# Feeding the down product's first operands at earlier places in the order of work

## The chip, the cores and the metric

The kernel runs on one core of a Trainium2 chip. The metric is the device time of one execution in microseconds (us). A core has five engines with queues of their own, which run each in its own order and wait for each other by semaphores: TensorE (PE, matmuls), VectorE (DVE), ScalarE (ACT), GpSimd (POOL) and SyncE (SP). SP and POOL here only start transfers (DMA) between the chip's large memory and the on-chip buffers. Matmuls write to eight accumulation banks ("bank"), from which VectorE and ScalarE read.

## The reference: two layers, each with a feed-forward block

The reference takes x (1024 positions by 1024 channels, float32) through two layers. Layer 0 mixes by a short gated convolution, layer 1 by a dilated attention. Behind each mixer comes the feed-forward block that matters here:

```python
def swiglu(h, w_gate, w_up, w_down):
    return (jax.nn.silu(h @ w_gate) * (h @ w_up)) @ w_down
...
        h = rms_norm(x, ffn_norm[i])
        x = x + swiglu(h, ffn_w_gate[i], ffn_w_up[i], ffn_w_down[i])
    return rms_norm(x, final_norm)
```

The inner width is 2816, 22 tiles of 128 rows.

## The kernel before

**Products in three parts.** Every float32 matrix is split into a high part (a rounded copy) and a low part (what is left), and a product is three matmuls: high by high, high by low, low by high (lines 505 to 507 in `mm`, 597 to 600 in `deeper`). The copy is made by ScalarE (line 137 for weights `w`, line 497 for operands `b`), and VectorE subtracts it to get the low part (lines 138 and 498). Each split so puts one instruction on ScalarE and one on VectorE.

**Seven products for eight.** The large products use Winograd's form of Strassen's scheme. A pair of weight tiles (a *unit*) is multiplied in seven products, m = 1, 2, 6, 5, 7, 3, 4 (`WINOGRAD`), and every product has an operand of its own made from the quarters of the activations, kept in `self.b[m]`. Gate and up have 22 units, 0 to 21. For units from 4 on, products 2 and 4 are themselves done by such a scheme on half-width pieces, for two units at a time; these are called *deep* products here, `(unit, DEEPER + i)` in the order of work, i = 1, 2, 5, 6, 7, 3, 4. After each deep product VectorE adds its two banks to stored parts (line 515).

**The order around the change.** `unit_order` writes it out by hand. At its end stand, for units 20 and 21: (20, 6), (20, 5), (20, 7), (21, 1), (20, 3), (21, 6), (21, 5), (21, 7), deep 1, deep 2, deep 5, deep 6, (21, 3), deep 7, deep 3, deep 4. Below, "sixth product", "fifth product" and so on mean (21, 6), (21, 5), and so on, by their number m and not by their place. A whole product is 12 matmuls of 512 columns, a deep one 12 of 256. Several products share one bank: deep 4 accumulates in the bank that deep 7 has filled, once VectorE has read it.

**The down product.** It reads the product of gate and up, of which 18 of the 22 tiles go through the seven-product scheme, in three chunks of three pairs. The quarters' sums were written to the large memory when they were made. `feed` (line 695) is a generator for one chunk: each call loads the three pieces of one operand (`hin`, line 702, on SP's queue) and then converts the three pieces loaded by the call before (ScalarE line 497, VectorE line 498), so eight calls load and convert all seven operands. `down` (line 719) then runs, for each m, the product for two output tiles, n and n + 2; after each VectorE adds the bank into the residual x (line 726), and the feed is called once. The products m = 1, 6, 7 and 4 share a bank: m = 6 can start only when m = 1's add has read it. Weights for down come by `load_raw` (line 151, SP's queue too) and are split a few products ahead by `ensure`.

**Where the feed starts.** The method `run` of class `Strassen` calls `filled(n)` after product number n of the gate and up order. Before the change, it calls the feed for the products of unit 21 that stand at deep 6 or behind it, five products.

**Buffers.** `hin`, the sums of weight tiles (`combo`), the parts of gate and up and some deep operands come from one pool of 20 half-page buffers; `b`, `w`, `raw` and `x` from 41 pages. A buffer that is written again waits for the last reader of what was in it. Instructions of each engine run in the order in which the program names them.

The block runs twice, once in each layer, with the same order of work.

Of the kernel before, what the change touches and what calls it, by code (L numbers as in the profile page):

```python
# [30 lines left out]
DEEP, DEEPER = (2, 4), 10  # L31
# [10 lines left out]
CONV = "conv"  # L42
# [52 lines left out]
def trunk(ctx: ExitStack, tc: tile.TileContext, x, gains_in, cwi, ck, cwo, wqkv, wo, relb,  # L95
# [62 lines left out]
    def ensure(upto):  # L158
        while op_state[0] < min(upto + 1, len(ops)):
            key = ops[op_state[0] + 1][0] if op_state[0] + 1 < len(ops) else None  # L160
            if key in sums_of:
                sums_of.pop(key)()
            made[op_state[0]] = ops[op_state[0]][1]()
            op_state[0] += 1
# [49 lines left out]
    def add_deep(unit, key, u, rows, upto):  # L214
# [27 lines left out]
        def early(op):  # L242
            w = op()
            run(*[sums_of(j, m) for j, m in enumerate(DEEP)])
            return w
# [105 lines left out]
    def run(*gens):  # L351
        for _ in zip(*gens):
            pass
        for g in gens:
            for _ in g:
                pass
# [6 lines left out]
    def both(w, ks, acts):  # L363
        banks = two_banks()
        run(product(w, ks, acts, banks))
        return banks
# [106 lines left out]
    class Strassen:  # L473
# [277 lines left out]
        def run(self, start, hooks={}):  # L751

            self.base = op_state[1]
            last = self.nu - 1

            def filled(n):
                start(n)
                if self.key != CONV:
                    self.now = n + 1
                    i = self.order.index((3, 4))  # L760
                    if n == i - 15:
                        prep.append(self.deepen(2))
                    if n == i - 5:
                        prep.append(self.deepen(4))
                    for p in prep:
                        next(p, None)
                if self.key == CONV:
                    self.below(n, last)
                else:
                    if self.order[n][0] == last and n >= self.at(last, DEEPER + 6) - self.base:  # L770
                        next(feed, None)
                    if self.order[n] == (last, DEEPER + 7):
                        self.load_x(0, 2)
                        ensure(self.at(last, DEEPER + 4) + 4)
                self.idle(n)

            prep = []
            if self.key == CONV:
                self.products(filled, hooks)
                self.first_tiles()  # L780
                return
            feed = self.feed(0)
            self.products(filled, hooks)
            for c in range(0, self.pairs, self.chunk):
                self.down(c, 0, feed)
                feed = self.feed(c + self.chunk) if c + self.chunk < self.pairs else self.feed_last()
                self.down(c, 4, feed)
            run(feed)


    class Conv(Strassen):
# [148 lines left out]
        def first_tiles(self):  # L940

            run(self.low)
            upper = self.halved(range(CO, KT))
            for n in range(KT):
                banks = two_banks()
                run(product(take(("co", 0, n), 2), range(CO), self.hid, banks))
                if n + 2 < KT:
                    self.load_x(n + 2)
                add_to_x(n, banks)
                self.step(4 if n < 2 else None)  # L950
                if n >= 3:
                    next(upper, None)
            run(upper)
            for f in range(CO):
                del self.plain[f]
# [843 lines left out]
```

## Time and profile before

| | us |
|---|---|
| median of three runs | 2215.94 |
| lowest and highest | 2215.3 and 2217.3 |
| profiled execution, its own time | 2215.37 |
| its span in the profile | 2213.6 |
| TensorE busy | 2143.2 (97%) |
| VectorE busy | 1769.8 (80%) |
| ScalarE busy | 998.4 (45%) |

How to read the rows. A row of a timeline gives the start in us from the span's begin, the duration, the engine, the line of the kernel, the operation, what it writes and reads by the program's names, how many instructions were merged, and in brackets the idle time of the engine ahead of it and what ended it. A row of waits gives who waited for whom: us in total, how often, the longest. Who ended a wait is inferred; where an instruction waits for several things, the one that came last by the profile is named. A row of windows gives a stretch, its length, for TensorE busy time and number of matmuls, the clock that was granted to TensorE (1.00 is full), the DMA engines' busy share and GB/s. On VectorE and ScalarE the instructions overlap a little: the time from one start to the next is shorter than the duration of one.

### The profile page before, as it was taken

How to read it: one execution, taken by the hardware profiler on the slowest of the kernel's cores; microseconds unless marked ns; L12 is line 12 of the kernel's file. 1: busy time of each engine (PE TensorE's matmuls, PEld its weight loads, DVE VectorE, ACT ScalarE, POOL GpSimd, SP SyncE). 2: the span in 40 equal slices, each digit the busy share in tenths (PEclk: the TensorE clock that was granted, in tenths of full speed). 3: DMA queues.
4: the chain of work that ended last, by engine and by line, in shares of the span. 5: the costliest groups of instructions: out<-in, count | busy, mean ns of one | idle time of the engine just before them, and what ended most of it. 6: DMA issues, size and time to landing. Idle time of an engine off the chain costs nothing.

```text
span 2213.6 us, 30526 instructions
## 1 busy us (share of the span) xinstructions
PE 2143.2 (97%) x11138; PEld 1829.8 (83%) x11138; DVE 1769.8 (80%) x3255; ACT 998.4 (45%) x1808; POOL 147.9 (7%) x196
## 2 busy tenths in 40 slices
PE   7899999899999999999999999999899999999998
PEld 5788887688888878878999999887678888878887
DVE  7797758888888798965677767868988888889886
ACT  6433425444444444434455555534534444444435
POOL 0000000010101000010111111110010101000000
PEclk9999999999999999999999999999999999999999
DMA  4122541222323374423333333544113323266432
GB/s 154 53 84 74 208 131 51 86 98 90 117 93 114 106 269 153 131 86 131 90 90 91 90 90 83 168 130 140 62 72 102 113 96 119 96 218 210 155 93 77
DMA packets 131263, 255.30 MB, mean 115 GB/s; under 512 B 47386, under 2 KB 58666, under 8 KB 131114
## 3 DMA queue, kind: packets, MB, share of 16 engines
q1 hardware_dynamic: 75978, 184.80, 26.2%
q0 software_dynamic: 13968, 45.46, 5.6%
q10 hardware_dynamic: 41168, 23.10, 3.6%
q8 instruction: 88, 1.44, 0.3%
q14 instruction: 61, 0.50, 0.1%
HBM read 187.04 MB, written 66.26 MB: 114 GB/s over the span
## 4 chain that ended last, share of the span: by engine, by line
PE 79%; DVE 11%; ACT 4%; DMA 3%; issue 2%; ACTq 0%; SPq 0%; DVEq 0%
PE bank L505 16%; PE bank L507 16%; PE bank L506 16%; PE bank L346 5%; PE bank L348 5%; PE bank L347 5%; PE bank L1425 4%; PE bank L600 2%; PE bank L599 2%; PE bank L597 2%; DVE b L498 2%; DVE w L138 2%; PE bank L1353 1%; PE bank L1352 1%; DVE x L438 1%
## 5 line engine op out<-in xcount | busy, mean ns | idle before, releaser
L505 PE MATMUL bank<-b,w 128*128 128x512 f32 x1784 | 706.1, 396 | 27.2 <-DVE part L515 7.3
L507 PE MATMUL bank<-b,w 128*128 128x512 f32 x1784 | 702.7, 394 | 15.8 <-DVE w L138 15.8
L506 PE MATMUL bank<-b,w 128*128 128x512 f32 x1784 | 702.7, 394 | 2.1 <-DVE b L498 2.1
L505 PEld LDWEIGHTS bank<-b,w 128*128 128x128 f32 x1784 | 339.8, 190 | 102.4 <-ACT w L137 10.5
L507 PEld LDWEIGHTS bank<-b,w 128*128 128x128 f32 x1784 | 339.4, 190 | 91.9 <-DVE w L138 20.3
L506 PEld LDWEIGHTS bank<-b,w 128*128 128x128 f32 x1784 | 340.0, 191 | 73.3 <-DVE b L498 2.9
L137 ACT ACTIVATE w<-combo 128x512 fp32r<-128x512 f32 (+2 forms) x464 | 235.0, 535 | 279.2 <-DVE combo L185 273.4
L138 DVE TENSOR_TENSOR w<-combo,w 128x512 fp32r<-128x512 f32 (+2 forms) x464 | 260.6, 575 | 69.2 <-ACT w L137 67.2
L511 ACT ACTIVATE part<-bank 128x512 f32<-128x512 f32 x168 | 99.2, 594 | 276.1 <-PE bank L507 273.6
L138 DVE TENSOR_TENSOR w<-raw,w 128x512 fp32r<-128x512 f32 (+2 forms) x316 | 168.9, 559 | 20.8 <-ACT w L137 19.1
L515 DVE TENSOR_TENSOR part<-part,bank 128x256 f32<-128x256 f32 (+1 forms) x348 | 158.6, 486 | 31.0 <-PE bank L507 15.5
L137 ACT ACTIVATE w<-raw 128x512 fp32r<-128x512 f32 (+2 forms) x316 | 150.2, 520 | 45.7 <-PE bank L507 11.3
L726 DVE TENSOR_TENSOR x<-x,bank 128x512 f32<-128x512 f32 x168 | 114.2, 680 | 30.9 <-PE bank L507 30.9
L346 PE MATMUL bank<-w_hi,w 128*128 128x512 f32 (+1 forms) x320 | 122.0, 381 | 0.0
L348 PE MATMUL bank<-w_hi,w 128*128 128x512 f32 (+1 forms) x320 | 120.0, 375 | 0.7 <-DVE w L138 0.7
L347 PE MATMUL bank<-w_lo,w 128*128 128x512 f32 (+1 forms) x320 | 119.8, 374 | 0.0
L438 DVE TENSOR_TENSOR x<-x,bank 128x512 f32<-128x512 f32 (+1 forms) x104 | 65.9, 641 | 62.6 <-PE bank L348 53.8
L185 DVE TENSOR_TENSOR combo<-raw 128x512 f32<-128x512 f32 (+1 forms) x160 | 102.9, 643 | 4.3 <-DMA raw<-in_conv_w_in 4.3
L346 PE MATMUL bank<-h_hi,w_hi 128*128 128x512 f32 x256 | 104.6, 409 | 0.7 <-ACT w_hi L137 0.7
L348 PE MATMUL bank<-h_hi,w_lo 128*128 128x512 f32 x256 | 100.2, 391 | 0.7 <-DVE w_lo L138 0.7
L347 PE MATMUL bank<-h_lo,w_hi 128*128 128x512 f32 x256 | 99.9, 390 | 0.0
L1111 ACT ACTIVATE part<-part 128x512 f32<-128x512 f32 x66 | 39.7, 628 | 110.6 <-DVE part L515 110.6
(237 smaller groups left out, 3835.2 us busy)
## 6 DMA issues: line engine op xcount, KB each, us to landing
hin<-part SPq DMA_DIRECT2D x126, 256.0 KB
raw<-in_ffn_w_gate SPq DMA_DIRECT2D x44, 512.0 KB
raw<-in_ffn_w_up SPq DMA_DIRECT2D x44, 512.0 KB
part<-sum POOLq DMA_DIRECT2D x72, 256.0 KB, 3.0
raw<-in_ffn_w_down SPq DMA_DIRECT2D x48, 384.0 KB
x<-spill SPq DMA_DIRECT2D x24, 512.0 KB
raw<-in_attn_w_qkv SPq DMA_DIRECT2D x24, 512.0 KB
raw<-in_conv_w_in SPq DMA_DIRECT2D x21, 512.0 KB
```

What stands on the lines that cost most here:

```text
L137: nc.scalar.activation(hi, src, AF.Copy)
L138: eng.tensor_tensor(out=lo, in0=src, in1=hi, op=ALU.subtract)
L185: eng.tensor_tensor(out=c, in0=a, in1=b, op=op)
L346: nc.tensor.matmul(b, whi[:, a], ahi[:, s], start=first, stop=False)
L347: nc.tensor.matmul(b, whi[:, a], alo[:, s], start=False, stop=False)
L348: nc.tensor.matmul(b, wlo[:, a], ahi[:, s], start=False, stop=last)
L505: nc.tensor.matmul(b, hi[:, a], bhi, start=start and k == 0, stop=False, skip_group_check=True)
L506: nc.tensor.matmul(b, hi[:, a], blo, start=False, stop=False, skip_group_check=True)
L507: nc.tensor.matmul(b, lo[:, a], bhi, start=False, stop=k == n - 1, skip_group_check=True)
L511: nc.scalar.activation(t, b, AF.Copy)
L515: nc.vector.tensor_tensor(out=t, in0=t, in1=b, op=ALU.add)
L726: nc.vector.tensor_tensor(out=X[n][:, half(h)], in0=X[n][:, half(h)], in1=b, op=ALU.add)
```

## The change

The feed of the first chunk is called at other places in the gate and up order of the last unit. Before, it was called after every product of unit 21 from deep 6 on. After, it is called after every product from (21, 6) on but deep 5 and deep 6; this takes in every entry of the order from there, and all of them belong to unit 21.

```diff
                 if self.key == CONV:
                     self.below(n, last)
                 else:
-                    if self.order[n][0] == last and n >= self.at(last, DEEPER + 6) - self.base:
+                    if n in feeding:
                         next(feed, None)
                     if self.order[n] == (last, DEEPER + 7):
                         self.load_x(0, 2)
...
             prep = []
+
+            feeding = [n for n, um in enumerate(self.order) if n >= self.order.index((last, 6))
+                       and um not in ((last, DEEPER + 5), (last, DEEPER + 6))] if self.key != CONV else ()
             if self.key == CONV:
```

The calls stand so, with what each one loads and converts:

| call | before, after | after the change, after | loads operand | converts operand |
|---|---|---|---|---|
| 1 | deep 6 | (21, 6) | 1 | - |
| 2 | (21, 3) | (21, 5) | 2 | 1 |
| 3 | deep 7 | (21, 7) | 6 | 2 |
| 4 | deep 3 | deep 1 | 5 | 6 |
| 5 | deep 4 | deep 2 | 7 | 5 |
| 6 | down, m = 1 | (21, 3) | 3 | 7 |
| 7 | down, m = 2 | deep 7 | 4 | 3 |
| 8 | down, m = 6 | deep 3 | - | 4 |

A ninth call, after deep 4, and those in the first part of the down product find the feed at its end and do nothing. The other chunks are fed as before.

## The prediction

> **What bounds the kernel now.** I read the page first, then the waits of TensorE (PE) in the two feed-forward blocks, then VectorE's (DVE) timeline there, then windows of busy time and clock.
>
> ```profile
> span 2213.6 us, 30526 instructions
> ...
> PE 2143.2 (97%) x11138; PEld 1829.8 (83%) x11138; DVE 1769.8 (80%) x3255; ACT 998.4 (45%) x1808; POOL 147.9 (7%) x196
> ...
> PE 79%; DVE 11%; ACT 4%; DMA 3%; issue 2%; ACTq 0%; SPq 0%; DVEq 0%
> ...
> part<-sum POOLq DMA_DIRECT2D x72, 256.0 KB, 3.0
> ```
>
> TensorE is busy 97% of the span and is 79% of the chain that ended last, so a change is worth what it does to TensorE's idle time. The place that the change touches has two idle stretches in each feed-forward block. TensorE's waits from 735 to 830 us and from 1925 to 2155 us, and the rows of the first pair:
>
> ```profile
> PE bank L505 <- ACT b L497: 3.0, 1, 3.0
> PE bank L597 <- DVE part L515: 2.0, 1, 2.0
> ...
> PE bank L505 <- ACT b L497: 3.0, 1, 3.0
> PE bank L597 <- ACT b L497: 2.0, 1, 2.0
> ```
>
> ```profile
> 786.21 0.36 PE L597 MATMUL bank<-t,w 128*128 128x256 f32 x1 [2.01 <-DVE part L515]
> ...
> 795.68 0.39 PE L507 MATMUL bank<-b,w 128*128 128x512 f32 x1
> 799.08 0.71 PE L505 MATMUL bank<-b,w 128*128 128x512 f32 x1 [3.01 <-ACT b L497]
> ```
>
> The first (2.01) stands before deep product 4 of the last unit, the second (3.01) before the down product's third step, m = 6 of output tile 0. Two releasers are named ACT b L497, a conversion of a later operand, on which nothing here depends. By the code, deep 4 accumulates in the bank that deep 7's add (L515) must have read, and m = 6 in the bank that m = 1's add into x (L726) must have read. VectorE's timeline agrees:
>
> ```profile
> 769.12 1.43 DVE L138 TENSOR_TENSOR w<-raw,w 128x256 fp32r<-128x256 f32 x4
> 770.48 0.75 DVE L138 TENSOR_TENSOR w<-combo,w 128x256 fp32r<-128x256 f32 x2
> 773.50 0.69 DVE L583 TENSOR_TENSOR c<-part,bank 128x512 f32<-128x512 f32 x1 [2.28 <-ACT part L511]
> 774.23 0.69 DVE L1114 TENSOR_TENSOR c<-c,c 128x512 f32<-128x512 f32 x1
> ...
> 777.38 0.74 DVE L515 TENSOR_TENSOR part<-part,bank 128x256 f32<-128x256 f32 x2
> 778.04 0.75 DVE L138 TENSOR_TENSOR w<-combo,w 128x256 fp32r<-128x256 f32 x2
> ...
> 781.38 0.69 DVE L515 TENSOR_TENSOR part<-part,bank 128x512 f32<-128x512 f32 x1 [0.59 <-PE bank L507]
> 782.10 0.69 DVE L1114 TENSOR_TENSOR part<-part 128x512 f32<-128x512 f32 x1
> 782.71 1.89 DVE L498 TENSOR_TENSOR b<-hin,b 128x512 fp32r<-128x512 f32 x3
> 784.51 1.22 DVE L138 TENSOR_TENSOR w<-raw,w 128x256 fp32r<-128x256 f32 x3
> 785.65 0.75 DVE L515 TENSOR_TENSOR part<-part,bank 128x256 f32<-128x256 f32 x2
> 786.32 1.89 DVE L498 TENSOR_TENSOR b<-hin,b 128x512 fp32r<-128x512 f32 x3
> ...
> 791.25 1.89 DVE L498 TENSOR_TENSOR b<-hin,b 128x512 fp32r<-128x512 f32 x3
> ...
> 794.92 1.89 DVE L498 TENSOR_TENSOR b<-hin,b 128x512 fp32r<-128x512 f32 x3
> ...
> 798.25 0.68 DVE L726 TENSOR_TENSOR x<-x,bank 128x512 f32<-128x512 f32 x1
> ```
>
> Deep 7's first add runs from 785.65 for half of 0.75 and TensorE goes on at 786.21; m = 1's add ends at 798.25 + 0.68 = 798.93 and TensorE goes on at 799.08, 0.15 later. Between 773.50 and 798.93 the reader sees one VectorE gap worth naming, 0.59 at 781.38. **VectorE, not a missing operand, is what TensorE waits for.** The four L498 rows are the low halves of operands 1, 2, 6 and 5; those of 7, 3 and 4 come after 798.93. The second block's queue ends alike, 1191.8 us later:
>
> ```profile
> 1990.02 0.68 DVE L726 TENSOR_TENSOR x<-x,bank 128x512 f32<-128x512 f32 x1
> ```
>
> The stall has a price behind it. TensorE in stretches of 3.4 us (busy, matmuls, granted clock):
>
> ```profile
> 795.73:799.14 3.41, 0.40 (x3) 1.00 1.02 372
> 799.15:802.55 3.40, 3.40 (x8) 0.50 1.02 415
> 802.60:806.00 3.40, 3.40 (x16) 1.00 0.35 141
> ...
> 1584.21:1587.60 3.39, 1.85 (x9) 1.00 0.00 0
> 1587.70:1591.00 3.30, 3.30 (x16) 1.00 0.42 103
> 1986.98:1990.39 3.41, 0.84 (x4) 1.00 1.03 297
> 1990.40:1993.80 3.40, 2.96 (x7) 0.50 1.01 408
> ```
>
> After 3.0 us of idle the clock is 0.50 for 3.4 us: 8 matmuls where 16 fit, a loss of 3.40 - 8 x 0.2125 = 1.70; in the second block 2.96 - 7 x 0.2125 = 1.47. After a stretch with 1.54 of idle (1584.21) it stays 1.00. So the two stalls cost 2.0 + 3.0 and about 1.6 of clock in each block.
>
> **The change, step by step.** It makes no instruction and takes none away: 21 loads (L702), 21 copies on ScalarE (ACT, L497) and 21 subtractions on VectorE (L498) per block stand at other places in the same queues. Before, the feed is called after deep 6, third product, deep 7, 3 and 4, then three times in the down product. After, it is called after the sixth, fifth and seventh product, deep 1 and 2, third product, deep 7 and 3. Operand 1 is so converted after the fifth product, 2 after the seventh, 6 after deep 1, 5 after deep 2, 7 after the third product, 3 after deep 7, 4 after deep 3.
>
> *VectorE.* One operand takes 784.51 - 782.71 = 1.80 us. Its queue is walked in program order, all work in it as measured:
> - Operand 1 comes behind the first two rows of the four at 769.12, about 769.8. The four other subtractions follow (1.4), and the queue would then be empty until 773.50. The 2.28 gap takes the 1.80 whole: it costs nothing. If the loads come late, this cover is gone and the 1.80 is on the path.
> - From 773.50 on the queue has no gap but the 0.59, which fills too.
> - Until deep 7's add come four more operands (2, 6, 5, 7) and not operand 1: 785.65 + 4 x 1.80 - 1.80 - 0.59 = 790.46. Half of 0.75 and 0.15 on, deep 4 starts near 791.0, not 786.21. The same backlog shows up earlier in TensorE as smaller waits at deep 6, the third product and deep 7 (deep 2's add, at 777.38 now, has two operands more ahead of it, 3.6).
> - Until m = 1's add into x come all seven operands, three more than now: 798.25 + 3 x 1.80 - 1.80 - 0.59 = 801.26. With 0.68 and 0.15, m = 6 starts at 802.1: **3.0 us later than 799.08**.
> - TensorE itself gets there in time: from deep 4 to the end of m = 2 took 786.21 to 796.07 (795.68 + 0.39), 9.9, and 791.0 + 9.9 = 800.9, then 1.2 of idle.
>
> After that point VectorE has 5.4 us less to do, three operands. TensorE's list of waits shows none behind 799.08 in the block, so this buys nothing. That is what the change trades: work taken from where nobody waited, put in front of an add for which TensorE waits.
>
> [...] Three rows in 1.89 say 0.60 from one to the next, since they overlap. [...]
>
> *ScalarE.* The 21 copies go forward with them; ScalarE is 45% busy and its copies come one operand ahead of VectorE. Nothing.
>
> *SP and the loads.* The loads move past the raw loads of down weights and the loads of x. By the code 15 of the 20 half-page buffers are held when operand 2 is loaded, so three loads go at once and two more; the sixth waits for operand 1's first subtraction (about 770.5). The first raw load stands behind it. Its rows now, and those of the loads that are late:
>
> ```profile
> 761.31 5.09 SPq L151 DMA_DIRECT2D raw<-in_ffn_w_down  x2
> ...
> 780.79 1.15 SPq L692 DMA_DIRECT2D x<-spill  x2
> ```
>
> ```profile
> 776.22 0.32 SPq L702 DMA_DIRECT2D hin<-part  x1
> ```
>
> ```profile
> 782.32 0.63 ACT L497 ACTIVATE b<-hin 128x512 fp32r<-128x512 f32 x1 [1.21 <-DMA hin<-part]
> 783.32 1.35 ACT L137 ACTIVATE w<-raw 128x384 fp32r<-128x384 f32 x3 [0.37 <-DMA raw<-in_ffn_w_down]
> ...
> 1971.73 1.65 ACT L497 ACTIVATE b<-hin 128x512 fp32r<-128x512 f32 x3
> ```
>
> That raw load, issued at 761.31, goes to about 771; its first use is at 783.32, so it has room. The two x loads of 780.79 fall behind operand 4's; m = 1's add reads them first, at 801. Loads of operands 6 and 5 wait for buffers that VectorE frees (by the walk 773 to 775.5, and 776.7 to 778). When they land no row shows; the bounds are a transfer of this size on POOL's queue, 3.0 (page, above), and the load issued at 776.22, for which ScalarE waits until 782.3: 6.1. Operand 5's last load, issued at 778, must have landed by 782.2: its subtraction is due after the rows from 773.50 to 778.04 (4.5), operands 2 and 6 (3.6) and two thirds of its own (1.2), at 782.8, less a 0.63 copy. With 3.0 it is on time, with 6.1 it is 1.9 late, and VectorE stands still behind it. Bounds 0 and 1.9 a block, no gain possible. I take 0.6, nearer to 0 since the raw loads that crowded that slow one are later now.
>
> *Clock.* The idle before m = 6 becomes 1.2 plus that lateness, 1.2 to 3.1. The rows above put the drop between 1.54 and 2.57 of idle in one 3.4 us stretch. On time there is no drop and 1.70 and 1.47 come back; late, none. I take half, 0.8 a block. Waits of up to 2 us earlier may drop the clock too, but TensorE has 1.2 to spare there.
>
> [...]
>
> Sum of a block: 3.0 + 0.6 - 0.8 = 2.8; two blocks 5.6. The profiled execution took 2215.37 (span 2213.6), which makes 2221.0; the median of the three runs, 2215.94, is 0.57 higher, so **2221.5**.
>
> **The rivals.**
> - *On time and at full clock.* Lateness 0, all clock back: 6.0 - 3.2 = 2.8, 2218.8, within 0.2% (4.4 us, about what a measurement of this kernel can tell from no change). For it: the second block's row at 1971.73 shows three copies that waited for no load. Against: buffers are short just there.
> - *No clock comes back.* The clock drops wherever m = 6 lands: 2 x (3.0 + 0.6) = 7.2, 2223.1. For it: 0.50 behind both stalls now. Against: 1.54 of idle did not drop it. [...]
> - *The waits go.* TensorE's labels name b L497 three times in four; if operands were the cause, both stalls vanish with the clock behind them: 2 x (2.0 + 3.0) + 3.2 = 13.2, 2202.7. Place: m = 6. The point from which it turns: VectorE must find more than 5.4 of idle time for the three operands ahead of L726, and by the walk it finds 1.80 + 0.59. [...]
> - *The change does not do what it says.* Buffers free so late (a POOL store must land first) that operand 6 stalls VectorE too, 2 to 5 us a block: 2226 to 2232. Against it: 20 buffers, of which VectorE frees one each 0.6 us.
>
> **How the numbers follow.** My forecast 0.36; no clock back 0.16; on time at full clock 0.27; the waits go 0.11; buffers too late 0.10. Slower by over 0.2% are the first two and the last, 0.62; same 0.27; faster 0.11. The range runs from full clock less 1 us of spread among runs, 2217.5, to 2 x (3.0 + 1.9) with no clock back, 9.8, 2225.7; it leaves out the waits going and most of the last. The slower cases' own: 2220.4 to 2225.7.
>
> **What would show it.** In the changed profile: L498 first near 770 inside the old 2.28 gap; no VectorE gap from there to L726; L726 at 801 to 803 relative to 773.50; TensorE waits before deep 6, the third product, deep 7, deep 4 and m = 6, each of 1 to 2.5; the granted clock in the 3.4 us behind m = 6 (1.00 or 0.50 settles the second term); a wait of VectorE or ScalarE on hin loads (settles the third). I am wrong if L726 comes before 799, or if TensorE waits behind m = 6 where it waits for nothing now.

## The result, and the profile after

The changed kernel takes 2220.72 us (median of 19 runs, 2218.22 to 2222.17), the kernel before, in as many runs beside it, 2216.03 (2213.68 to 2217.83). The ratio is 1.0020, with a 95% interval of 1.0014 to 1.0026: slower by 3.1 to 5.8 us. The forecast was 2221.5. The profiled execution took 2221.45, that of before 2215.37.

The page of the profile after, its span and its busy times:

```profile
span 2219.6 us, 30519 instructions
...
PE 2144.6 (97%) x11138; PEld 1830.2 (82%) x11138; DVE 1771.2 (80%) x3255; ACT 1000.1 (45%) x1808; POOL 147.6 (7%) x196
```

The work is the same, the span 6.0 longer. To see where, I took the rows of VectorE and ScalarE that stand in both traces, and how much later each is after than before: 0.18 ahead of the first place of the change (700 to 750), 2.71 behind it (850 to 1000), 3.27 ahead of the second (1900), 5.53 behind it (2050 to 2200). The change so costs 2.53 in the first feed-forward block and 2.26 in the second. The rest lies where nothing was changed: 0.18 ahead of the first place, 0.56 between the two blocks, and the remainder behind the last of these rows; executions differ by that much.

TensorE's waits in the changed kernel, from 735 to 830 us and from 1925 to 2155:

```profile
PE bank L597 <- ACT w L137: 3.4, 1, 3.4
PE bank L597 <- DVE part L515: 3.2, 2, 1.8
PE bank L505 <- ACT w L137: 0.2, 1, 0.2
...
PE bank L597 <- DVE part L515: 3.2, 2, 1.8
PE bank L597 <- ACT w L137: 3.1, 1, 3.1
PE bank L505 <- ACT w L137: 0.2, 1, 0.2
```

Two waits of 2.0 and 3.0 have become four, of 1.3, 0.2, 3.4 and 1.8. VectorE's timeline at the place (start, duration, operation, number of instructions, idle time ahead):

```profile
770.13 1.90 DVE L498 TENSOR_TENSOR b<-hin,b 128x512 fp32r<-128x512 f32 x3
...
773.68 0.69 DVE L583 TENSOR_TENSOR c<-part,bank 128x512 f32<-128x512 f32 x1 [0.31 <-ACT part L511]
...
784.14 0.69 DVE L498 TENSOR_TENSOR b<-hin,b 128x512 fp32r<-128x512 f32 x1 [0.97 <-ACT b L497]
...
786.75 1.34 DVE L515 TENSOR_TENSOR part<-part,bank 128x256 f32<-128x256 f32 x3
...
791.68 0.75 DVE L515 TENSOR_TENSOR part<-part,bank 128x256 f32<-128x256 f32 x2
...
802.49 0.68 DVE L726 TENSOR_TENSOR x<-x,bank 128x512 f32<-128x512 f32 x1
```

ScalarE's copy ahead of the row of 784.14:

```profile
783.47 0.63 ACT L497 ACTIVATE b<-hin 128x512 fp32r<-128x512 f32 x1 [1.50 <-DMA hin<-part]
```

And TensorE's:

```profile
787.31 0.36 PE L597 MATMUL bank<-t,w 128*128 128x256 f32 x1 [3.36 <-ACT w L137]
...
792.24 0.38 PE L597 MATMUL bank<-t,w 128*128 128x256 f32 x1 [1.84 <-DVE part L515]
...
803.26 0.40 PE L507 MATMUL bank<-b,w 128*128 128x512 f32 x1
803.50 0.40 PE L505 MATMUL bank<-b,w 128*128 128x512 f32 x1
```

What to see: operand 1 lies in the old gap, of which 0.31 is left. Then VectorE's queue is full but for 0.97 before the last piece of operand 5, whose copy on ScalarE waited for its load. Deep 1, 6, 7 and 4 accumulate in the same banks, one after the other, and each can start only when the adds of the one before have read them. Deep 7 starts 0.15 after the first add of deep 6 has ended (786.75 + 0.41 for one of its instructions), and deep 4 as long after deep 7's first add (791.68 + 0.41): the two large waits are for VectorE's adds, although the first is labelled with a conversion of weights. The add of m = 1 into x comes at 802.49. From the row of the fifth product (773.68) that is 28.80, where it was 798.25 - 773.50 = 24.75. But TensorE doesn't wait for it: m = 6 starts at 803.50, right behind the matmul of 803.26 and 0.33 after the add ends. TensorE itself was late. The clock tells why (stretches of 3.41 us: TensorE's busy time and matmuls, granted clock):

```profile
782.20:785.61 3.41, 1.75 (x8) 1.09 (x6) 2.44 (x6) 2.14 (x6) 0.00 (x0) 1.00 0.99 315
785.61:789.03 3.42, 1.72 (x14) 1.75 (x15) 3.38 (x9) 3.42 (x9) 0.00 (x0) 1.00 1.03 395
789.03:792.44 3.41, 1.57 (x14) 1.40 (x12) 3.41 (x9) 2.89 (x6) 0.54 (x1) 1.00 1.05 405
792.44:795.85 3.41, 3.41 (x15) 3.22 (x15) 3.38 (x7) 0.80 (x2) 0.00 (x0) 0.50 1.02 407
```

The slow stretch that stood behind m = 6 now stands in deep 4 and m = 1.

### The profile page after: what moved, and what is told of

Read it like the earlier page. It is cut to its first block, busy times and chain, and to the rows that moved or that the text cites. A ratio compares the mean times of both kernels' runs of the same rounds, so it can differ in the third digit from the quotient of the medians.

```text
span 2219.6 us, 30519 instructions
## 1 busy us (share of the span) xinstructions
PE 2144.6 (97%) x11138; PEld 1830.2 (82%) x11138; DVE 1771.2 (80%) x3255; ACT 1000.1 (45%) x1808; POOL 147.6 (7%) x196
## 4 chain that ended last, share of the span: by engine, by line
PE 54%; issue 25%; DVE 11%; ACT 4%; DMA 3%; POOL 2%; ACTq 0%; SPq 0%; POOLq 0%; DVEq 0%
PE bank L507 10%; PE bank L505 10%; PE bank L506 10%; PE bank L348 5%; PE bank L346 5%; PE bank L347 4%; PE bank L1428 4%; DVE w L138 2%; DVE b L498 1%; POOL part L687 1%; PE bank L1356 1%; PE bank L1355 1%; DVE x L438 1%; POOL part L668 1%; DVE acc L400 1%
```

## The experiments

**Theory.** VectorE works through its queue in order; each operand's three subtractions that are put ahead of an add for which TensorE waits delay that add by 1.80, and each taken away brings it forward by as much. **Rival.** What costs is the early loads: few buffers are free, other loads are under way, operands come late. The kernels below are told by the products of unit 21 (`last`; `last - 1` is unit 20) after which the feed is called, and by the steps m of the first down tiles after which it is called. Six of them are the kernel before with another list; four have a further edit, which is told of with them, and two are repeats. The first edit stands for all of them:

```diff
-                    if self.order[n][0] == last and n >= self.at(last, DEEPER + 6) - self.base:
+                    if self.order[n] in feeding:
                         next(feed, None)
...
+            feeding = [(last, m) for m in (6, 5, DEEPER + 7, DEEPER + 3, DEEPER + 4,)]
             feed = self.feed(0)
...
-                next(feed, None)
+                if c or n or m in (1, 2, 6):
+                    next(feed, None)
```

### One operand ahead

> The feed is called after the sixth and the fifth product, and then after deep 7, 3, 4 and three steps of the down product: operand 1 is converted early, all others where they stood before. Theory (VectorE's queue ahead of an add is what TensorE waits for): operand 1 falls into VectorE's old gap of 2.28 us and leaves the stretch behind it, so deep 7's add and m = 1's add into x both come 1.80 us earlier than before; deep 4 starts with hardly a wait (0.2 to 0.5), m = 6 starts 1.80 earlier, its wait stays near 3.0 and so does the slow clock behind it: 2 x 1.80 off, 2212.4. Rival (what costs is that loads of operands are started early, among the loads of weights and with few buffers free): the six loads now stand early too, and the time is 2216 or more.

Measured: 2211.43 (11 runs; 2216.15 before), ratio 0.9979 (0.9970 to 0.9988). TensorE's waits in the first block, and VectorE's two rows:

```profile
PE bank L505 <- ACT b L497: 3.0, 1, 3.0
PE bank L597 <- DVE part L515: 0.2, 1, 0.2
```

```profile
772.84 0.69 DVE L583 TENSOR_TENSOR c<-part,bank 128x512 f32<-128x512 f32 x1 [0.32 <-ACT part L511]
...
795.78 0.68 DVE L726 TENSOR_TENSOR x<-x,bank 128x512 f32<-128x512 f32 x1
```

From row to row it is 22.94 where it was 24.75: 1.81 less, in both blocks, and later work moved forward by 1.78 and 1.80 a block. Six loads stand as early as in the change, and cost nothing. The theory holds to 0.02. The median went down by 4.7, 1.1 more than 3.6. The two profiled executions, 2215.37 and 2211.85, differ by 3.5, so that no trace places this part; executions of one kernel differ by more (2213.68 to 2217.83 for the kernel before).

### Operand 5 behind

```diff
+            feeding = [(last, m) for m in (DEEPER + 6, 3, DEEPER + 7, DEEPER + 3,)]
...
+                if c or n or m in (1, 2, 6, 5):
```

> The kernel before, with the feed's call after deep 4 moved to the fourth step of the down product: operands 5, 7, 3 and 4 come one call later, nothing comes earlier. Theory (VectorE's queue): one operand fewer stands ahead of m = 1's add into x, which comes 1.80 earlier; deep 4 still waits 2.0; m = 6 waits 1.2 in place of 3.0, and with so short a wait the clock stays 1.00 behind it: 1.80 + 1.70 in the first block, 1.80 + 1.47 in the second, 6.8 off, 2209.2. If the clock drops all the same, 3.6 off, 2212.4. Rival (a missing operand is what TensorE waits for): operand 5 is ready later, and TensorE waits for it at m = 5: 2216 or more.

Measured: 2211.78 (11 runs), ratio 0.9980 (0.9971 to 0.9989): 4.4 off, not 6.8. The add came 1.81 earlier (22.94 again) and the clock stayed 1.00 behind m = 6, as expected. TensorE's rows show what took the rest:

```profile
796.34 0.47 PE L505 MATMUL bank<-b,w 128*128 128x512 f32 x1 [1.21 <-ACT b L497]
...
805.15 0.47 PE L505 MATMUL bank<-b,w 128*128 128x512 f32 x1 [0.40 <-ACT b L497]
...
810.03 0.47 PE L505 MATMUL bank<-b,w 128*128 128x512 f32 x1 [0.55 <-ACT b L497]
```

Two waits that the kernel before doesn't show now stand before m = 7 and m = 3. They are for VectorE too: each ends 0.14 after an add into x has ended (804.33 + 0.68 and 809.21 + 0.68). From start to start, with the slower first matmul behind each, they cost 0.64 and 0.79, about 1.4, and the clock gave back 1.58 (below): 1.81 + 1.58 - 1.4 = 2.0 a block, and the trace shows 1.96 and 1.82. The slow clock had hidden them: they hang on the clock, since the kernel with one operand ahead, which keeps the clock of 1.00 behind m = 6 in its second block alone, has them there (0.37 and 0.55) and not in the first.

### Both edits

```diff
+            feeding = [(last, m) for m in (6, 5, DEEPER + 7, DEEPER + 3,)]
...
+                if c or n or m in (1, 2, 6, 5):
```

> Both edits: operand 1 converted in VectorE's old gap, operands 5, 7, 3 and 4 one call later than before. Theory (VectorE's queue): m = 1's add into x comes 3.6 earlier, deep 4 starts 1.8 earlier, m = 6 waits about 1.2 and the clock stays 1.00: (3.6 + 1.70) + (3.6 + 1.47) = 10.4 off, 2205.6. Rival (loads and operands): no better than the better one of its two edits alone.

Measured: 2208.97 (5 runs), ratio 0.9963 (0.9951 to 0.9976), 7.2 off. The rival, no better than one edit alone (2211.4), is out. VectorE's rows:

```profile
772.53 0.69 DVE L583 TENSOR_TENSOR c<-part,bank 128x512 f32<-128x512 f32 x1 [0.32 <-ACT part L511]
...
793.66 0.68 DVE L726 TENSOR_TENSOR x<-x,bank 128x512 f32<-128x512 f32 x1
```

21.13: 3.62 less than before, two times 1.81. The 3 us that are short of the forecast are the same two waits, 0.37 and 0.55, in both blocks, at about 1.4 a block as above.

### The change with its last three operands put back

```diff
+            feeding = [(last, m) for m in (6, 5, 7, DEEPER + 1, DEEPER + 2,)]
...
+                if c or n or m in (1, 2, 6):
```

> The changed kernel, with its last three calls of the feed put back into the down product: operands 1, 2, 6 and 5 come as early as in the change, 7, 3 and 4 where they stood before. Theory (VectorE's queue): m = 1's add into x is rid of three operands (802.5 - 5.4 = 797.1), but deep 7's add still has operands 2, 6 and 5 ahead of it, so deep 4 starts at about 790.4 and TensorE comes to m = 6 at 800.3 to 801.7 without a wait there; no slow clock behind m = 6: 2214.6 to 2217.4, so about as before, and 3 to 6 below the changed kernel. Rival (the three early operands 7, 3 and 4 are harmless, the early loads cost): as the changed kernel, 2220 to 2221.

Measured: 2214.57 (11 runs), ratio 0.9994 (0.9985 to 1.0003). That is 6 below the changed kernel, although TensorE didn't wait for m = 1's add in the changed kernel, and fifteen of the 21 loads stand as early as there. Of the three operands, 7 stood ahead of deep 7's add in the change, and deep 4 waited 1.8 for that add. Now neither deep 4 nor m = 6 is among the waits of the first block:

```profile
PE bank L597 <- DVE part L515: 4.3, 2, 3.0
PE bank L505 <- ACT w L137: 0.5, 1, 0.5
```

The waits that are left, 1.3 before deep 6 and 3.0 before deep 7, come from operands 2, 6 and 5, which this kernel has as early as the change. The profiled execution is the longest of a wide spread (2211.9 to 2217.3): its second block has two slow stretches.

### GpSimd makes the low halves

```diff
-                    lows = [self.hi(last, k, t, nc.vector)
+                    lows = [self.hi(last, k, t, nc.gpsimd)
```

> The changed kernel, with the 21 subtractions of the low halves of the first chunk (and those of the second chunk, by the same line) on GpSimd in place of VectorE: loads, copies and the order stay those of the change. Theory (VectorE's queue ahead of the adds): VectorE has 12.6 us less to do ahead of and behind m = 1's add, so the waits before deep 6, deep 7 and deep 4 go, and none comes at m = 6; if GpSimd takes no more than about 4 us for the three subtractions of an operand, 2203 to 2208. If it takes longer, the operands come late, and TensorE's waits stand at the beginning of down steps instead, for an operand; the adds on VectorE still come earlier than in the kernel before. Rival (the early loads are what costs): the waits before deep 7 and deep 4 stay, 2219 to 2222.

Measured: 2254.91 (4 runs), ratio 1.0177 (1.0163 to 1.0191). Both sides missed. In these blocks GpSimd otherwise only starts transfers; in attention, from 1073 to 1480 us, it has sixteen PARTITION_ALL_REDUCE as well. GpSimd's, VectorE's and TensorE's rows:

```profile
796.45 11.04 POOL L498 TENSOR_TENSOR b<-hin,b 128x512 fp32r<-128x512 f32 x9
```

```profile
795.49 12.42 DVE L138 TENSOR_TENSOR w<-raw,w 128x256 fp32r<-128x256 f32 x3
807.84 0.74 DVE L515 TENSOR_TENSOR part<-part,bank 128x256 f32<-128x256 f32 x2
```

```profile
808.39 0.55 PE L597 MATMUL bank<-t,w 128*128 128x256 f32 x1 [11.22 <-DVE part L515]
```

Nine subtractions in a row take GpSimd 11.04. Of VectorE's three the third begins at 796.16, 0.29 before them, and ends at 807.91, 0.42 after them, where two such take 0.75 in other rows. Deep 7's add stands behind it and deep 4 behind the add. Here VectorE stood through the work, in one instruction of 11.75, for longer than it would have taken itself for it (9 x 0.60 = 5.4). The run doesn't settle what it was made for, but it is one more add held back by 11, and TensorE waited 11.2 for it.

### Two operands ahead

```diff
+            feeding = [(last, m) for m in (1, 6, 5, DEEPER + 3,)]
...
+                if c or n or m in (1, 2, 6, 5):
```

> As the kernel with both edits, with operand 2 ahead too: the feed is called after the last unit's first, sixth and fifth product, after deep 3, and after four steps of the down product, so operands 1 and 2 are converted in the two gaps of VectorE before 773.5 (1.22 and 2.28 us for 3.6 us of work). Theory (VectorE's queue): m = 1's add into x comes 1.7 earlier than with one operand ahead, the waits before deep 4 (0.2) and m = 6 (1.2) go, and the waits of 0.4 and 0.55 behind m = 6 stay or shrink by up to 0.5: 1.4 to 2.0 a block below that kernel, 2205 to 2206 beside its 2209.0. Rival (an earlier start collides with loads, pages or ScalarE's work for TensorE): TensorE waits before 780 where it waits for nothing now, and the time is 2209 or more.

Measured: 2208.75 (5 runs), ratio 0.9964 (0.9951 to 0.9976): no better than the kernel with both edits (2208.97), which has one operand ahead. Here the rival has its case. VectorE's row of operand 2's last piece, and TensorE's waits up to 800:

```profile
772.58 0.69 DVE L498 TENSOR_TENSOR b<-hin,b 128x512 fp32r<-128x512 f32 x1 [1.12 <-ACT b L497]
```

```profile
PE bank L597 <- DVE part L515: 1.3, 2, 1.1
PE bank L597 <- ACT w L137: 0.3, 1, 0.3
PE bank L600 <- DVE w L138: 0.3, 1, 0.3
```

The wait before m = 6 is gone, but the piece's load started only at 768.40, when operand 1's first subtraction had given its buffer back. VectorE stood 1.12, and TensorE waits that long before deep 6.

### More buffers

```diff
-PAGES = 41
+PAGES = 40
...
-        scope["halves"] = 20
+        scope["halves"] = 22
```

> The changed kernel with 22 half-page buffers in the last stage in place of 20, and 40 pages in place of 41 throughout, which makes the room. Only the second feed-forward block has the added buffers. If operand 5 is late (VectorE stood 0.97 before its last subtraction) because its loads wait for buffers, that idle time goes in the second block, and deep 7, deep 4 and m = 6 come up to 1.0 earlier there than in the changed kernel; the time is 2219 to 2220. If the transfers themselves are slow, the idle time stays: 2220 to 2221.5. In the first block nothing changes, unless the missing page is missed.

The kernel that ran has 22 half pages in the first stage too, so both blocks show the effect. Measured: 2226.35 (5 runs), ratio 1.0046 (1.0032 to 1.0059), slower than the change and outside both forecasts. By the trace the blocks are not what makes it slower: 3.0 are lost before 200 us and 3.9 between 1100 and 1700. The missing page is the likely cause there, which no run shows alone. VectorE's rows in the first block:

```profile
776.49 0.69 DVE L583 TENSOR_TENSOR c<-part,bank 128x512 f32<-128x512 f32 x1 [0.32 <-ACT part L511]
...
804.17 0.68 DVE L726 TENSOR_TENSOR x<-x,bank 128x512 f32<-128x512 f32 x1
```

27.68, and 27.69 in the second block; the prediction's walk without any late load gave 801.26 - 773.50 = 27.76. With 20 buffers it was 28.80 and 28.39 in the change, and 28.19 and 27.82 in the execution told of below. So late pieces cost 1.1, 0.7, 0.5 and 0.1, and nothing with two buffers more. That fits buffers as the cause, with four blocks against two. And even so a block takes 1.41 and 1.45 more than before the change: with the loads in time, the order on VectorE still costs.

### Sooner, and later still

```diff
+            feeding = [(last - 1, 7), (last - 1, 3), (last, 5), (last, DEEPER + 3)]
...
                 if tiles:
+                    self.b[last] = [None] * self.chunk
...
                 if m:
-                    self.b[m] = [None] * self.chunk
                     yield
```

> Two operands ahead as in the kernel before this one, but with the loads and the conversion of operand 1 sooner: the feed is called after the seventh and third product of the unit before the last, after the last unit's fifth product, after deep 3 and after four steps of the down product. Operand 1 is then converted in VectorE's gap of 1.22 and gives its three buffers back sooner, so operand 2's loads are out sooner. Theory (operand 2's third piece came 1.12 late for want of a buffer): TensorE's wait of 1.1 before deep 6 goes, 1 us a block, 2206 to 2207 beside 2208.8. Rival (operand 1 falls where VectorE has no room, or ScalarE's copies for it hold up what TensorE reads): a new wait of 0.5 to 2 us before 775, 2208 to 2212.

The second edit lets go of gate and up's operand only when the new one is converted, since (21, 1) still reads operand 1 when the loads for its successor are started. Measured: 2206.83 (5 runs), ratio 0.9956 (0.9942 to 0.9970). The wait before deep 6 is gone. Operand 2's three pieces follow each other, but operand 1 lies behind the gap of 1.22 and not in it. TensorE waits 0.34 for ScalarE, whose copies of operand 1 (1.66 from 767.96) stand ahead of a save:

```profile
770.67 0.50 PE L505 MATMUL bank<-b,w 128*128 128x512 f32 x1 [0.34 <-ACT part L511]
```

So both sides have a part, the theory the larger. The other side of the stretch, with the list of both edits and the steps 1, 6, 5 and 7 in place of 1, 2, 6 and 5:

> The kernel with both edits (operand 1 ahead, 5 behind), with operands 7, 3 and 4 one step of the down product later still: the feed is called after the last unit's sixth and fifth product, deep 7, deep 3, and the steps m = 1, 6, 5 and 7. Theory (VectorE's queue): the waits of 0.37 and 0.55 before m = 7 and m = 3 stand behind the adds of m = 6 and m = 5, which have one operand fewer ahead of them (1.80), so both go: 0.9 to 1.4 a block, 2206 to 2207 beside 2209.0. Rival (operands come too late now): a load has only about 4 us of a step until its copy, and loads took 3 to 6: TensorE waits 1 to 3 us for an operand before m = 7, 3 or 4, 2210 to 2216.

Measured: 2206.28 (5 runs), ratio 0.9957 (0.9945 to 0.9970). TensorE's waits in the first block:

```profile
PE bank L505 <- ACT b L497: 1.2, 1, 1.2
PE bank L506 <- DVE b L498: 0.4, 1, 0.4
PE bank L597 <- DVE part L515: 0.2, 1, 0.2
```

The two waits behind m = 6 are gone; 0.4 stands before m = 7's second matmul, which reads an operand's low half: there operand 7 comes late, as the rival had it, at a small price. Then the two together, two operands ahead with the sooner loads, and the steps 1, 6, 5 and 7:

> The two best orders together: operands 1 and 2 ahead in VectorE's two gaps, with the sooner loads, and operands 5, 7, 3 and 4 after the steps m = 1, 6, 5 and 7. Theory (VectorE's queue): neither m = 6 nor m = 3 waits, there remain 0.35 before the last unit's seventh product, 0.2 before deep 4 and 0.4 before m = 7's second matmul, 0.3 to 0.6 a block below the better of the two: 2205 to 2206. Rival (the later operands now come too late, since TensorE is at m = 7 up to 1.2 sooner): the wait at m = 7 grows to 1 or 1.5, 2206 to 2208, no better than either.

Measured: 2205.37 (5 runs), ratio 0.9957 (0.9943 to 0.9971). The waits listed are down to these, in both blocks:

```profile
PE bank L505 <- ACT part L511: 0.3, 1, 0.3
PE bank L597 <- DVE part L515: 0.2, 1, 0.2
```

By the trace it gains 5.0 and 4.9 a block, against 4.6 and 4.4, and 4.2 and 4.0 of the two it joins; the three can't be told apart by their times. All are faster than both kernels.

### The two kernels once more

> The kernel before once more, to see another execution of it in the profile. Theory (the clock is set by what TensorE did in the stretch before, on a grid of 3.413 us whose phase differs from execution to execution): the slow stretches lie on a grid of another phase; the stall of 3.0 us before m = 6 drops the clock only where at least 1.85 of it fall into one stretch, the stall of 2.0 before deep 4 now and then. Rival (the clock answers to the length of a stall): the same two slow stretches, right behind the end of both stalls of 3.0.

> The changed kernel once more. The same waits by the theory of VectorE's queue (1.3, 0.2, 3.3, 1.8, none before m = 6), since they do not hang on the clock; the slow stretches by the grid's phase: behind the stall of 3.4 if 1.85 or more of it fall into one stretch of the grid, else behind the one of 1.8 or nowhere. If there is no slow stretch in deep 4 and m = 1, TensorE comes to m = 6 about 1.4 sooner and waits 0.8 to 1.4 there. Rival (length of a stall): slow again from 792.4.

Measured: 2216.49 and 2219.48, one run each. The waits of the kernel before are the same to 0.02. The changed one waits 1.3, 0.6, 2.4, 1.8 and again not at m = 6; the wait before deep 7 is 1.0 shorter than in the first execution, and VectorE's 0.97 before operand 5's last piece is absent (0.35 stands before operand 6's). The clock of the kernel before (first block):

```profile
793.68:797.09 3.41, 1.13 (x5) 0.58 (x4) 3.38 (x8) 0.38 (x1) 0.84 (x2) 1.00 0.99 345
797.09:800.50 3.41, 2.67 (x6) 2.15 (x7) 3.41 (x7) 3.41 (x8) 0.00 (x0) 0.50 1.01 394
800.50:803.91 3.41, 3.41 (x9) 2.63 (x8) 3.41 (x8) 1.21 (x3) 0.00 (x0) 0.50 0.57 231
```

It was slow for two stretches here and for one in the first profile, after the same stall, and that cost 1.2 more. The place of the slow stretches in these two executions doesn't part the theories, since they stand behind the same products. The kernel with one operand ahead does, in its second block, where m = 6 waits 3.0 as well:

```profile
1982.46:1985.87 3.41, 1.87 (x9) 1.21 (x7) 3.38 (x7) 0.00 (x0) 1.08 (x2) 1.00 0.91 244
1985.87:1989.28 3.41, 1.94 (x9) 1.63 (x10) 3.41 (x7) 3.06 (x7) 0.00 (x0) 1.00 0.94 344
1989.29:1992.70 3.41, 3.41 (x17) 2.81 (x16) 3.41 (x8) 1.94 (x4) 0.00 (x0) 1.00 1.04 417
```

The stall falls half into one stretch and half into the next, 1.54 and 1.47 of idle, and the clock stays 1.00; in the first profile of before 3.01 fell into one stretch (795.73), and the next had 0.50. Between these two it isn't the stall's length that sets the clock, but how much of it falls into one stretch.

## Why the prediction was right, and where not

- **"VectorE, not a missing operand, is what TensorE waits for."** Shown. One operand less ahead of m = 1's add is 1.81 earlier, two are 3.62, in every block tried. The labels that name conversions are wrong at these waits.
- **"3.0 us later."** The three operands ahead, less what the gaps take, are 24.75 to 27.76 by the walk, 27.68 in the kernel whose loads were not late. The term is right to 0.1. Operand 1 is free, as said, in the changed kernel and alone.
- **"I take 0.6"** for late loads: 1.1, 0.7, 0.5 and 0.1 in four blocks, 0.6 on average. The bounds of 0 and 1.9 held.
- **"I take half, 0.8 a block"** of the clock: this term was mis-sized. At m = 6 all of it came back in all four blocks. It is 1.58, not 1.70, in the first block of before: a matmul takes 0.2275 at full clock in these rows, not 0.2125, so 3.40 - 8 x 0.2275.
- **"Then 1.2 of idle"** before m = 6 was wrong, and with it the reasoning that this wait decides the clock. TensorE came later than 800.9 plus lateness: behind the wait of 1.84 before deep 4 the clock was 0.50 for 3.41 us, which takes up all the idle time. The prediction named that possibility and that the idle time would pay for it, and it paid nearly all: m = 6 starts 0.18 after it could have (802.49 + 0.68 + 0.15 = 803.32).
- **The sum of a block.** First block: 4.05 (VectorE and late pieces) + 0.18 - 1.58 = 2.65, and 2.53 was measured. It was forecast as 2.8, from 3.0 + 0.6 - 0.8. That the two lie so near is in part luck: more came late in this block than was taken (1.1 against 0.6), and more clock came back (1.58 against 0.8). Second block: 3.64 + 0.19 - 1.37 = 2.46, and 2.26 was measured; here too the prediction's 1.47 of clock is 2.96 - 7 x 0.2275 = 1.37. In the four blocks of the change that were profiled, work behind the place is 2.53, 2.26, 1.91 and 1.71 later than in the first profile of before.
- **The waits named.** Forecast: five, "each of 1 to 2.5". There are four: 1.3, 0.2, 3.4 and 1.8. Deep 7's is longer by operand 5's late piece, and m = 6's is missing.
- **The rivals.** "The waits go" is out: the add comes 3 to 4 later. "Buffers too late" is out as a large cost and right as a small one. "On time at full clock" (2218.8) had the clock right and the lateness wrong; "no clock comes back" (2223.1) had the clock wrong. The measured 2220.7 lies between the forecast and the former.

## What to carry to other kernels

In these runs an add of VectorE came 1.81 earlier for each operand taken from ahead of it, and later for what was put ahead of it and no gap took, whatever wait that was meant to shorten: first walk the engine's queue and count what gap takes the moved work. Here the gap took one operand of seven, so one operand early gained 1.8 a block, and three more ahead of the add than before put that add 2.9 later (27.68 against 24.75). The best order put work early only into gaps, and the rest behind the adds for which TensorE waits.

## What the runs showed that was not expected

**The slow stretches lie on a grid.** In every profile all slow stretches begin on a grid of 3.413 us, of one phase within an execution, which differs between executions: those of the two blocks begin at 799.14 and 1990.40 in the first profile of before (349 steps of 3.4134 apart), at 797.09 and 1991.76 in the second (350 of 3.4133). From the place of the change to the end of each feed-forward block (735 to 970 and 1925 to 2170), over all profiles, of the stretches at full clock with 1.1 us of idle or more, the clock dropped behind all twelve with 1.99 or more, behind none of the 27 with 1.70 or less, and behind five of the seven with 1.82 to 1.87. So a stall of 1.84 cost as much clock (0.50 for the 3.41 us behind it, in the changed kernel) as one of 3.0 in the first profile of before, and one of 3.4 in the changed kernel or of 3.0 in the kernel with one operand ahead nothing (1.00), by where it fell; behind the same stall the two profiled executions of the kernel before had one slow stretch and two. Elsewhere less idle was enough, where TensorE ran small matmuls in the rest of the stretch. The clock dropped behind these two rows of before, to 0.50 from 334.93 and from 983.46, after stretches with 1.32 of idle and with none:

```profile
333.44 1.05 PE L417 MATMUL bank<-ones,acc 128*128 128x1 f32 x8 [1.32 <-DVE acc L400]
...
980.42 2.59 PE L456 MATMUL bank<-oh,rel 33*16 33x512 f32 x8
```

So idle time by the rows is not the whole of what the clock goes by; what is stays open.

**VectorE stood through several of GpSimd's instructions.** This was in the kernel with the low halves on GpSimd. The subtraction that VectorE began at 796.16 took 11.75, until nine of GpSimd, 1.25 each and back to back, were through; one from 780.47 took 5.38, through four. It was not always so in this run: from 852.73 GpSimd ran fifteen in 23.13, about 1.5 each, and VectorE's instructions came in between them, none taking more than 1.65. What decides between the two is not shown.
